# Conditioning loads on GpSimd's queue and a reordered recurrence stage in a two-layer hybrid decoder trunk

## The chip, the cores and the metric

The kernel runs on one core of one Trainium2 chip. The metric is the time of one execution on the device in microseconds; the time of a kernel is the median of its runs.

## The reference

Two layers, each of three sub-layers: a half-step SwiGLU FFN, a token mixer, another half-step FFN. Layer 0 mixes with HGRN2 (a gated linear recurrence), layer 1 with a chunked causal gMLP. Every sub-layer is wrapped by a norm before and after, with shift, scale and gate from a conditioning vector c. All is float32; SEQ is 256, D_MODEL 1024, D_FF 2816.

```python
def sublayer(x, fn, pre_g, post_g, shift, scale, gate, res_w):
    h = rms_norm(x, pre_g) * (1.0 + scale) + shift
    return x + res_w * gate * rms_norm(fn(h), post_g)

def swiglu(h, w_in, w_out):
    a, b = jnp.split(h @ w_in, 2, axis=-1)
    return (jax.nn.silu(a) * b) @ w_out

def hgrn2_mix(h, w_in, w_out, out_norm, lb):
    q, f, i, g = jnp.split(h @ w_in, [HG_F, 2 * HG_F, 2 * HG_F + D_MODEL], axis=-1)
    q = jax.nn.silu(q)
    log_f = jnp.logaddexp(jnp.log(lb), jnp.log1p(-lb) + jax.nn.log_sigmoid(f))
    k = (1.0 - lb) * jax.nn.sigmoid(-f)
    # S_t = diag(f_t) S_{t-1} + k_t i_t^T,  o_t = S_t^T q_t, in chunks, 8 heads of 128
    ...
    o = rms_norm(o, out_norm) * jax.nn.silu(g)          # per head
    return o.reshape(B, S, D_MODEL) @ w_out

cond = jax.nn.silu(c)
mod = cond @ ada_w[i] + ada_b[i]      # per layer: 9 x 1024 shifts, scales and gates
```

## The kernel before

**Weights.** They come in 188 blocks of 128x2048 float32 (1 MB), in the order in which they are used. `wblock` (L112) loads a block in two halves into `raw` tiles over SP's queue and splits it into a high part (cast on ScalarE, L119) and a low part (subtraction on VectorE, L120), both in the float32r format; each product of full precision is then three TensorE products of high and low parts (`mm3`, `mm3f`, `chunk2`). Six split blocks fit in the pool `whl` (12 tiles), which in the recurrence stage also holds the gate `gg`, the values `v`, the keys `kn` and the decays with queries `bq`.

**Conditioning.** `ada_w` is 144 tiles of 128x1024 (512 KB). `ada` (L159) loads each and reduces it against `cond` on VectorE (L169) into a column of `mod`. The loads go through `self.load` (L55), which writes them into SP's queue in program order between the weight halves; `pace` sets how many go with each block. Their buffers are the pool `adap` (two tiles), and for the first 16 also four tiles of `p4`. The norm gate of a sub-layer (`gate_tile`, L188) is the only user of GpSimd's (POOL's) queue: a row is stored to DRAM and read back to all partitions, `gflat` and `G`, once for each of the six sub-layers.

**Order on the engines.** The kernel is written in program order; the build's planner then orders each engine's instructions by when it takes their inputs to be ready, earlier program text first, and gives out buffers. What must not move is tied by hand: `keep_in_program_order` ties an instruction to the one traced before it on its engine, and `paced` ties a product behind the one named in `self.gate`.

**FFNs.** The first accumulates block by block as its conditioned input appears (L418). The other three begin with two units in token-major form (`proj`, split order, L291 to L294, then `post_tok`: silu, product, transposes L396, split into `gT`), and run nine further units of 256 columns (`unit2`, `chunk2`, L328 and L329), with the output products (`out_unit`, L142 to L144) of a unit two behind them.

**The recurrence stage, `hgrn`.** The projections come in this order: first half of the gate with the first half of the values (`proj`), queries and forget gates of the first four heads (`feat`, L334 to L336), then, as fill between the steps of the first four heads' recurrence, queries and forget gates of the other four and the second half of the values (`tok`). `gate_f` (L524) turns a forget projection into log decays and keys, a chain between ScalarE and VectorE with a scratch tile `L` from the pool `adap`. `attn` (L551) is the recurrence of four heads in nine steps: the diagonal scores (L559), seven levels of block size 64 down to 1 (operands L582, L587, L593 on VectorE with an exponential between, scores L599, merge L570), and the products with the values (L632, L634). `zip_steps` puts one step of the fill behind each step of `attn`. `finish` (L639) norms the heads of a half (squares with a sum per head on ScalarE, L645; scaling and gating per head on VectorE, L658), transposes them (L663) and splits them for the output products. The second half of the gate is projected as fill of the second `attn`.

## Time and profile before

| | us |
|---|---|
| runs, median of 3 | 1191.67 (1189.63 to 1193.36) |
| the profiled execution | 1193.24, span 1191.5 |
| TensorE busy | 1146.5 |
| VectorE busy | 888.8 |
| ScalarE busy | 657.2 |
| GpSimd busy | 6.8 |
| idle VectorE ended by a conditioning load | 91.5 (51 times) |
| issue to landing, conditioning load on SP's queue, median | 6.5 |
| mean granted TensorE clock | 0.984 |

The stages by the trace: first FFN to about 218 us, recurrence 218 to 386, second FFN to 575, third to 770, gMLP to 1000, last FFN to the end. In the views PE is TensorE's products, PEld its weight loads, DVE VectorE, ACT ScalarE, POOL GpSimd, SP the queue that issues loads; L120 is line 120 of the kernel. A row of waits names who waited for whom, with total, times and longest in us. A matmul's busy time includes its overlap with the next one.

### The profile page before, as it was taken

The page shows a single profiled execution, that of the slowest core. Times are in us where ns is not written, and L with a number is a line of the kernel's source. Part 1 is how long each engine was busy: PE and PEld are TensorE (multiplying, and loading weights), DVE is VectorE, ACT ScalarE, POOL GpSimd, SP SyncE. Part 2 cuts the span into 40 slices and gives each one's busy share as a digit, 9 for nine tenths or more (in the row PEclk, how much of TensorE's full clock was granted, in tenths as well). Part 3 has the DMA queues.
Part 4 walks back from the last instruction along what each step waited for, and adds up shares of the span by engine and source line. Part 5 has one row for each costly group of instructions (what it writes and reads, how often), then busy time and mean ns, then how long its engine had stood idle before and what let it go on. Part 6 is the DMA issues. An engine that isn't in the chain of part 4 may idle for free.

```text
span 1191.5 us, 17180 instructions
## 1 busy us (share of the span) xinstructions
PE 1146.5 (96%) x6518; PEld 995.4 (84%) x6518; DVE 888.8 (75%) x1331; ACT 657.2 (55%) x1054; POOL 6.8 (1%) x16
## 2 busy tenths in 40 slices
PE   7999999997997999999999999999999999999997
PEld 6999998797895788888778888888888887888886
DVE  6997888868887887787677787657978786666652
ACT  6464446648766754456655545554754457555541
POOL 0000000000000000000000000000000000000000
PEclk9999999997999999999999999999999999999999
DMA  9899998782335777887578888537777765666640
GB/s 345 311 314 318 333 327 314 251 285 101 124 95 185 263 267 272 278 272 262 173 251 267 282 269 272 188 124 261 277 254 262 248 212 177 203 222 233 213 137 36
DMA packets 79765, 282.32 MB, mean 237 GB/s; under 512 B 9873, under 2 KB 10561, under 8 KB 79682
## 3 DMA queue, kind: packets, MB, share of 16 engines
q1 hardware_dynamic: 78626, 278.05, 68.0%
q0 software_dynamic: 1056, 3.17, 0.8%
q8 instruction: 51, 0.84, 0.3%
q14 instruction: 32, 0.26, 0.1%
HBM read 280.11 MB, written 1.07 MB: 236 GB/s over the span
## 4 chain that ended last, share of the span: by engine, by line
PE 73%; DMA 10%; DVE 8%; ACT 5%; issue 3%; SPq 0%; DVEq 0%; ACTq 0%
PE ups L328 15%; PE ups L329 8%; PE y L144 7%; PE y L142 7%; PE y L143 7%; PE ups L418 4%; DMA ada<-in_ada 4%; DMA raw<-in_wffn 4%; DVE w L120 3%; PE ups L334 3%; PE ups L336 3%; PE ups L335 3%; DMA raw<-in_whg 3%; ACT w L119 2%; PE ab L599 2%
## 5 line engine op out<-in xcount | busy, mean ns | idle before, releaser
L120 DVE TENSOR_TENSOR w<-raw,w 128x1024 fp32r<-128x1024 f32 x376 | 453.5, 1220 | 84.7 <-ACT w L119 77.5
L119 ACT CAST w<-raw 128x1024 fp32r<-128x1024 f32 x376 | 388.0, 1050 | 202.9 <-DMA raw<-in_wffn 79.4
L328 PE MATMUL ups<-h,w 128*128 128x512 f32 x864 | 303.1, 394 | 0.0
L169 DVE CUSTOM_DVE_ANT_0 junkv<-ada,cond 128x1024 bf16<-128x1024 f32 x144 | 175.8, 1221 | 92.0 <-DMA ada<-in_ada 91.5
L329 PE MATMUL ups<-h,w 128*128 128x256 f32 x864 | 242.5, 281 | 0.0
L328 PEld LDWEIGHTS ups<-h,w 128*128 128x128 f32 x864 | 162.3, 188 | 36.8
L142 PE MATMUL y<-w,t 128*128 128x512 f32 x448 | 179.4, 400 | 4.5 <-ACT t L147 4.5
L143 PE MATMUL y<-w,t 128*128 128x512 f32 x448 | 178.2, 398 | 0.0
L144 PE MATMUL y<-w,t 128*128 128x512 f32 x448 | 177.6, 397 | 0.2
L329 PEld LDWEIGHTS ups<-h,w 128*128 128x128 f32 x864 | 163.7, 190 | 0.9
L334 PE MATMUL ups<-h,w 128*128 128x256 f32 x416 | 118.3, 285 | 0.6 <-ACT w L119 0.6
L336 PE MATMUL ups<-h,w 128*128 128x256 f32 x416 | 117.8, 283 | 0.2 <-DVE w L120 0.2
L335 PE MATMUL ups<-h,w 128*128 128x256 f32 x416 | 117.6, 283 | 0.0
L142 PEld LDWEIGHTS y<-w,t 128*128 128x128 f32 x448 | 84.5, 189 | 24.1 <-ACT t L147 5.3
L144 PEld LDWEIGHTS y<-w,t 128*128 128x128 f32 x448 | 84.3, 189 | 21.0 <-DVE t L148 1.1
L143 PEld LDWEIGHTS y<-w,t 128*128 128x128 f32 x448 | 84.5, 189 | 17.9
L79 ACT ACTIVATE t<-t 128x256 f32<-128x256 f32 (+2 forms) x70 | 36.3, 523 | 97.7 <-DVE t L378 95.5
L334 PEld LDWEIGHTS ups<-h,w 128*128 128x128 f32 x416 | 79.7, 192 | 1.7 <-ACT w L119 0.8
L335 PEld LDWEIGHTS ups<-h,w 128*128 128x128 f32 x416 | 79.7, 192 | 0.8 <-issue 0.2
L336 PEld LDWEIGHTS ups<-h,w 128*128 128x128 f32 x416 | 79.7, 192 | 0.4 <-DVE w L120 0.4
L291 PE MATMUL pps<-w,h 128*128 128x512 f32 x160 | 64.4, 403 | 5.3 <-DVE h L247 5.3
L292 PE MATMUL pps<-w,h 128*128 128x512 f32 x160 | 63.8, 399 | 0.0
(199 smaller groups left out, 1435.4 us busy)
## 6 DMA issues: line engine op xcount, KB each, us to landing
raw<-in_wffn SPq DMA_DIRECT2D x264, 512.0 KB, 5.5
ada<-in_ada SPq DMA_DIRECT2D x144, 512.0 KB, 6.5
raw<-in_wgmu SPq DMA_DIRECT2D x48, 512.0 KB, 5.2
raw<-in_whg SPq DMA_DIRECT2D x40, 512.0 KB, 5.8
raw<-in_wgmv SPq DMA_DIRECT2D x24, 512.0 KB, 5.0
G<-gflat POOLq DMA_DIRECT2D x6, 512.0 KB, 5.9
t<-in_gbin SPq DMA_DIRECT2D x6, 256.0 KB, 5.2
x<-in_x SPq DMA_DIRECT2D x2, 512.0 KB, 4.0
```

Of the source, the lines that this page charges most:

```text
L119: nc.scalar.copy(hi[:, sl], raw)
L120: nc.vector.tensor_sub(lo[:, sl], raw, hi[:, sl])
L142: self.paced(mm(ps, l[0], r[0], start=start, stop=False))
L143: mm(ps, l[0], r[1], start=False, stop=False)
L144: mm(ps, l[1], r[0], start=False, stop=stop)
L169: nc.vector.tensor_tensor_reduce(junk, t, self.cond, 1.0, 0.0, ALU.mult, ALU.add, self.mod[i // 24][:, i % 24:i % 24 + 1])
L291: mm(res[g][t], h(0, kc), u(0, kc), start=kc == 0, stop=False)
L328: self.paced(mm(ps, u[0], self.h2[:, :, :, kc, :], start=kc == 0, stop=False))
L329: mm(ps[:, 1, :], u[1], self.h2[:, 0, :, kc, :], start=False, stop=kc == KC - 1)
L334: self.paced(mm(o, u[0], h[0], start=start, stop=False))
L335: mm(o, u[0], h[1], start=False, stop=False)
L336: mm(o, u[1], h[0], start=False, stop=stop)
```

## The change

- The conditioning loads are issued on GpSimd's queue, tied to the order of that queue. `adap` has three tiles. The scratch `L` of `gate_f` has a tile of its own for one pair of heads and uses the tile `hf` for the other.
- `pace` spreads the loads over 22, 23 and 27 blocks where it spread them over 25, 26 and 30; in the later FFNs it is set before `post_tok`.
- In the later FFNs the first half of the first `unit2` is written between the two token tiles of `post_tok`, and each group of output products is tied behind the last unit product.
- In the recurrence stage both halves of the gate are projected first, with silu at eviction; then the forget gate of the first four heads; then the queries of all eight. The first recurrence is filled with half of the first values, the other forget gate, the rest of the first values and a quarter of the second values, two steps ahead; the second with the rest of the values and the output products. The weight blocks are laid out in that order, and the step behind the diagonal scores is tied behind them.
- `finish` squares a whole bank, sums the four heads of it on VectorE, multiplies with the gate before the norm's factor is known, and scales by that factor per head.

```diff
-        self.adap = pool("adap", 2)
+        self.adap = pool("adap", 3)
+        self.lp = pool("lp", 1)
...
-            self.load(t, self.d["ada"][i])
+            self.tc.keep_in_program_order(nc.gpsimd.dma_start(t, self.d["ada"][i]))
...
     def out_unit(self, y, gT, wo, first):
         for t in range(NT):
             for h in range(2):
+                self.gate = self.last
...
         def post_tok(pa, pb):
             gTs = [self.gtile() for _ in range(2)]
+            pend.extend(gTs)
...
-            return gTs
+                yield
...
-            pend = post_tok(*self.proj(hT, [wa, wb], 512, split=True))
+            pend = []
+            self.pace(bg, 23)
+            tokens = post_tok(*self.proj(hT, [wa, wb], 512, split=True))
+            next(tokens)
+            steps = unit2(nb(), nb())
+            next(steps)
+            next(tokens)
...
-            L = self.adap.tile([P, 512], F32, tag="ada", name="L")
+            L = self.lp.tile([P, 512], F32, tag="L", name="L") if pr else self.scr.tile([P, 512], F32, tag="hf", name="L")
...
         def finish(hb, ops, sqrt=False):
...
             for u in range(2):
-                for i in range(4):
-                    junk = self.scr.tile([P, 512], BF16, tag="junka", name="junka")
-                    nc.scalar.activation(junk[:, 0:P], o4[u][:, i, :], AF.Square, accum_out=ss[:, 4 * u + i:4 * u + i + 1])
+                o3 = ops[u].rearrange("p t h v -> p (t h) v")
+                sq = self.t2().rearrange("p (i v) -> p i v", i=4)
+                nc.scalar.activation(sq, o3, AF.Square)
+                c0 = 2 * (2 * hb + u) * P
+                nc.vector.tensor_mul(og[:, 512 * u:512 * u + 512].rearrange("p (t c) -> p t c", t=NT),
+                                     ops[u].rearrange("p t h v -> p t (h v)"), gg[:, :, c0:c0 + 2 * P])
+                nc.vector.reduce_sum(ss[:, 4 * u:4 * u + 4], sq, axis=mybir.AxisListType.X)
...
                 for i in range(4):
-                    t, c0 = i // 2, (2 * pair + i % 2) * P
-                    nc.vector.scalar_tensor_tensor(on[:, i, :], o4[u][:, i, :], r[:, 4 * u + i:4 * u + i + 1],
-                                                   gg[:, t, c0:c0 + P], op0=ALU.mult, op1=ALU.mult)
+                    nc.vector.tensor_scalar(on[:, i, :], on[:, i, :], r[:, 4 * u + i:4 * u + i + 1], None, op0=ALU.mult)
...
         for t in range(NT):
-            self.tact(gg[:, t, 0:512], pg[0][t], AF.Silu)
-            nc.scalar.copy(v[:, t, 0:512], pg[1][t])
+            for g in range(2):
+                self.tact(gg[:, t, 512 * g:512 * g + 512], pg[g][t], AF.Silu)
...
-        run(feat(lambda pr, ps: self.tact(qs(0, pr), ps, AF.Silu)))
         self.table("natural_log_exp_and_others")
         self.hg_cols()
         run(feat(lambda pr, ps: gate_f(0, pr, ps)))
+        self.table("silu_and_others")
+        for hb in range(2):
+            run(feat(lambda pr, ps: self.tact(qs(hb, pr), ps, AF.Silu)))
+        self.table("natural_log_exp_and_others")
...
         zip_steps(attn(0, bank_y, ops[0]), [
-            feat(lambda pr, ps: nc.scalar.copy(qs(1, pr), ps)), once(q1_silu),
-            feat(lambda pr, ps: gate_f(1, pr, ps)),
-            tok(lambda t, ps: nc.scalar.copy(v[:, t, 512:], ps))], 5)
+            once(v0), once(v0), feat(lambda pr, ps: gate_f(1, pr, ps)), v0, once(v1)], 2)
...
         def outs():
             finish(0, ops[0])
             yield
+            yield
...
-        zip_steps(attn(1, bank_a, ops[1]), [
-            tok(lambda t, ps: nc.scalar.copy(gg[:, t, 512:], ps)), outs()], 0)
+        zip_steps(attn(1, bank_a, ops[1]), [v1, outs()], 0)
         y = state["y"]
-        self.table("silu_and_others")
-        g_silu(1)
```

More of the change, by code (lines that the diff above doesn't have):

```diff
@@ L328, in chunk2 @@
             self.paced(mm(ps, u[0], self.h2[:, :, :, kc, :], start=kc == 0, stop=False))
-            mm(ps[:, 1, :], u[1], self.h2[:, 0, :, kc, :], start=False, stop=kc == KC - 1)
+            self.last = mm(ps[:, 1, :], u[1], self.h2[:, 0, :, kc, :], start=False, stop=kc == KC - 1)
         return ps
@@ L335, in mm3f @@
         mm(o, u[0], h[1], start=False, stop=False)
-        mm(o, u[1], h[0], start=False, stop=stop)
+        self.last = mm(o, u[1], h[0], start=False, stop=stop)
     def gtile(self):
@@ L434, in ffn @@
             else:
-                steps = unit2(nb(), nb())
-                next(steps)
+                if u > 2:
+                    steps = unit2(nb(), nb())
+                    next(steps)
                 next(steps)
@@ L558, in attn @@
                     c = slice(512 * u + i * P, 512 * u + (i + 1) * P)
-                    nc.tensor.matmul(ps[:, i * P:(i + 1) * P], k[:, c], q[:, c], start=True, stop=True)
+                    score = nc.tensor.matmul(ps[:, i * P:(i + 1) * P], k[:, c], q[:, c], start=True, stop=True)
+                self.gate = score
                 nc.vector.tensor_mul(St[:, 512 * u:512 * u + 512].rearrange("p (i t) -> p i t", i=4),
@@ L679, in bank_a, with once @@
             return self.acc.tile([P, 512], F32, tag="acc", name="ab")
-        def g_silu(g):
-            o = gg[:, :, g * 512:(g + 1) * 512]
-            self.tact(o, o, AF.Silu)
-        def once(fn):
-            fn()
-            return
-            yield
+        def once(gen):
+            yield next(gen)
         def run(*gens):
@@ L1056, in _layout @@
     bl = []
-    for c0 in (3072, 2048, 0, 1024, 512, 1536, 2560, 3584):
-        bl += [_blk(hw, (512 * h, 512), (c0, 512)) for h in range(2)]
+    for c0, h in ((3072, 0), (3072, 1), (3584, 0), (3584, 1), (1024, 0), (1024, 1), (0, 0), (0, 1), (512, 0), (512, 1),
+                  (2048, 0), (1536, 0), (1536, 1), (2048, 1), (2560, 0), (2560, 1)):
+        bl.append(_blk(hw, (512 * h, 512), (c0, 512)))
     bl += [_blk(ho, (256 * u, 256), (0, D)) for u in range(4)]
```

22 lines of the change are left out of this document (10 added, 12 removed).

## The prediction

> **What bounds the kernel now.** I read the page first: engine totals, then the chain that ended last.
>
> ```profile
> span 1191.5 us, 17180 instructions
> PE 1146.5 (96%) x6518; PEld 995.4 (84%) x6518; DVE 888.8 (75%) x1331; ACT 657.2 (55%) x1054; POOL 6.8 (1%) x16
> PE 73%; DMA 10%; DVE 8%; ACT 5%; issue 3%; SPq 0%; DVEq 0%; ACTq 0%
> ```
>
> TensorE is busy for 96% of the span and carries 73% of the chain. The change leaves its number of products nearly as it is, so the gain can come only from the 45 us in which PE stands, and from stretches in which it runs at half clock. The second view is therefore PE's waits, over hgrn (260 to 375 us) and then over what follows (400 to 1030 us).
>
> ```profile
> PE ots L663 <- DVE t L658: 4.4, 1, 4.4
> PE fps L336 <- DVE w L120: 3.1, 2, 1.7
> PE ab L599 <- DVE t L593: 3.0, 1, 3.0
> PE fps L334 <- ACT w L119: 0.7, 1, 0.7
> PE ab L634 <- DVE t L570: 0.5, 1, 0.5
> ...
> PE y L142 <- ACT t L147: 4.5, 3, 2.4
> PE tps L396 <- DVE t L393: 0.9, 1, 0.9
> ```
>
> The columns are: who waited for whom, microseconds in total, times, longest. The first five rows are the recurrence's stage; the last two are the token-major start of the three later FFNs, one wait each. The third view cuts the span into stretches (PE, PEld, DVE, ACT, POOL busy, then granted clock, DMA share, GB/s).
>
> ```profile
> 0.00:16.00 16.00, 7.43 (x21) 4.44 (x21) 6.79 (x17) 10.51 (x16) 0.20 (x4) 1.00 0.87 317
> 16.00:64.00 48.00, 48.00 (x383) 47.62 (x384) 43.86 (x71) 25.84 (x37) 0.00 (x0) 0.96 0.91 324
> 64.00:163.00 99.00, 99.00 (x692) 92.35 (x691) 80.96 (x107) 48.25 (x55) 0.78 (x2) 1.00 0.92 327
> 314.00:364.00 50.00, 49.38 (x328) 44.05 (x326) 42.20 (x70) 33.26 (x69) 0.12 (x1) 1.00 0.36 118
> ...
> 273.20:280.05 6.85, 5.50 (x26) 5.50 (x27) 5.84 (x10) 6.74 (x13) 0.00 (x0) 0.50 0.64 227
> 286.87:293.70 6.83, 6.83 (x34) 6.83 (x34) 3.83 (x9) 6.03 (x16) 0.00 (x0) 0.50 0.26 85
> 363.50:372.20 8.70, 4.17 (x14) 2.61 (x13) 6.79 (x16) 6.33 (x13) 0.00 (x0) 0.80 0.73 250
> ```
>
> The first FFN (16 to 163 us) has PE full and the DMA engines at 0.91: nothing can be won there, only lost. Inside hgrn two stretches after idle PE time ran at clock 0.50, and a third has a mean of 0.80.
>
> **The change, what it should take away.** A: gate, forget and query order. Today the first forget gate's ACT and VectorE work falls beside query products of the second half, and its scratch tile L shares the two conditioning buffers:
>
> ```profile
> ACT L L529 <- DVE mod L169: 3.9, 1, 3.9
> SPq L56 <- DVE mod L169: 77.2, 42, 6.2
> ```
>
> SP, whose queue carries the weights too, stood 77.2 us for conditioning buffers; that goes, and where PE is full it brings nothing. ACT stood 3.9 us for a conditioning reduction to free L, and weight casts (L119) queue behind it on ACT, L120 behind them, PE behind those. After the change L has buffers of its own, two query products (2 x 96 products of 256 columns, at 48.0/383 = 0.125 us, 24 us) follow the first gate as cover, and the level-64 operands are ready before the scores. So the waits of 3.1, 0.7 and 3.0 go: 6.8 us. The half-clock stretches behind them: 26 and 34 products at 0.125 would take 3.25 and 4.25 us where 5.50 and 6.83 were busy, 4.8 us. A = 11.6 us. What is late next is VectorE in the recurrence, costed under F.
>
> B: whole-bank output norm before the last products.
>
> ```profile
> L645 ACT ACTIVATE junka<-ab x16: 251/278/280, 327.0 to 365.1; 128x128 bf16<-128x128 f32 x16
> L645 ACT ACTIVATION_READ_ACCUMULATOR junka<-ab x16: 186/194/205, 327.1 to 365.3; 128x1 f32 x16
> L658 DVE SCALAR_TENSOR_TENSOR t<-ab,r,w x16: 337/342/353, 342.4 to 369.6; 128x128 f32<-128x128 f32 x16
> L393 DVE TENSOR_TENSOR t<-t,pps 128x512 f32<-128x512 f32 x6 | 4.1, 680 | 0.6 <-PE pps L294 0.6
> L79 ACT ACTIVATE t<-pps 128x512 f32<-128x512 f32 x6 | 3.5, 587 | 0.0
> L233 DVE TENSOR_SCALAR xn<-x,r 128x512 f32<-128x512 f32 x10 | 4.8, 485 | 0.3
> ```
>
> Of the stretch 363.5 to 372.2 us, 14 products need about 2.4 us at full clock (6 of 512 columns at twice 0.125, 8 transposes at 0.11, the pitch of the small scores under F); 6.3 us are lost. Eight squares with their accumulator reads, 8 x (0.278 + 0.194) = 3.8 us on ACT, become two of 0.59. VectorE gets two products of 0.68, two reductions, and eight scalings of 128x128 instead of eight of 0.342. No row shows such a reduction: bounds 0.485 (L233) and 0.68 (L393), taken 0.68 because it reads as L393 does, a whole bank at one element a step. A 128x128 scaling lies between a quarter of L233 (0.12) and L658 (0.342); taken 0.25. The path to the first transpose is then one square 0.59, one reduction 0.68, three column operations of 0.2, four scalings 1.0: 2.9 us, with one weight cast and one subtraction possibly ahead (1.05 + 1.22) 5.2. PE has 12 output products (3.0 us) beside it, so 0 to 2.2 us of idleness stay, plus an ACT pass of 0.59 that evicts the transposes; I take 1.8. B = 6.3 - 1.8 = 4.5 us (bounds 3.5 to 5.7). The table switch and the second half's gate silu that stood ahead of it on ACT go too; ACT was covered there, so I give nothing for them.
>
> C: FFN starts. Output products that ran ahead of their order (L142 waiting for L147) are now held behind the last unit product, and the first half unit of the next block (16 products of 512 columns and 16 of 256, 6.0 us) fills between the two token halves. 4.5 + 0.9 = 5.4 us; I leave 0.4 for what stays. C = 5.0 us.
>
> **What it adds.** The 144 conditioning loads leave SP's queue for POOL's, behind the norm-gate transfers only.
>
> ```profile
> L169 DVE CUSTOM_DVE_ANT_0 junkv<-ada,cond 128x1024 bf16<-128x1024 f32 x144 | 175.8, 1221 | 92.0 <-DMA ada<-in_ada 91.5
> L461 DVE TENSOR_TENSOR lb_m<-lb x1: 156/156/156, 70.8 to 70.8; 128x8 f32<-128x8 f32 x1
> L201 POOL DMA_DIRECT2D G<-gflat x6: 550/551/560, 162.9 to 1140.0; - x6
> DMA to landing us min/median/max: 3.5/6.5/11.1
> DMA to landing us min/median/max: 4.3/5.9/7.5
> 263.00:380.00 117.00, 0.66 (x1) 0.93 0.41 139
> 380.00:537.00 157.00, 33.01 (x27) 0.98 0.76 261
> ```
>
> L461 belongs to hgrn and ran at 70.8 us, as soon as its input was there: the build's planner runs ahead whatever is ready. The loads were paced because SP's queue is written in order. On POOL each waits only for one of three buffers and for the POOL instruction before it, so they will run in bursts, each burst stopped by the next gate's pair of transfers (POOL stands there for the landing, 4 to 7 us, and the loads behind it with it; no reduction is due then). Issue costs 144 x 0.55 = 79 us of a POOL that is 1% busy. The last two rows are the reductions alone: 27 lie in 380 to 537 us; by the code's counts 24 of those are issued between the second and the third gate's transfers and can now start at about 315 us, inside the second recurrence.
>
> D, start: the loads compete with x. Up to seven (four ring, three own buffers) leave at once; x and constants are 1.16 MB, at 317 GB/s 3.7 us, and if both queues take turns the second x lands up to 3.7 us late, against about 1.5 us of slack (issued within the first 2 us and 4.0 to landing, so near 6; used at 7.55). PE at 16 to 64 us is full, so a late start stays. Bounds 0 and 3.7; I take 1.2, nearest the row of the use.
>
> ```profile
> x<-in_x SPq DMA_DIRECT2D x2, 512.0 KB, 4.0
> ...
> 6.32 1.22 DVE xn L905
> 7.55 1.14 DVE yg L905
> ```
>
> The Trainium skill, page "DMA: Bandwidth & Descriptors", section "Rules for kernel authors", speaks against this part: issuing from several engines gives no bandwidth, since all share 16 DMA engines. With that rule D is the 1.2 us taken; were the queues independent it would be 0 and the sum 1.2 lower. The share of 0.87 at the start agrees with the rule.
>
> E, bursts in the second recurrence: 24 reductions want 24 x 1.30 = 31 us where VectorE has 50.0 - 42.2 = 7.8 us idle, so about six fit, each pushing the next VectorE instruction by up to 1.3 us. Bounds -1 (those six no longer stand in the next stage) and 7.8; PE has fill there, so I take 2.
>
> F, the recurrence itself: per level VectorE does
>
> ```profile
> L582 DVE TENSOR_TENSOR t<-w 128x512 f32<-128x512 f32 x12 | 8.2, 683 | 0.2 <-issue 0.2
> L593 DVE TENSOR_TENSOR t<-t,w 128x512 f32<-128x512 f32 x14 | 9.7, 690 | 0.2 <-ACT t L79 0.2
> L570 DVE COPY_PREDICATED t<-lmask,ab 128x512 f32<-128x512 int32 x14 | 12.5, 893 | 4.9 <-PE ab L599 4.9
> 295.09 1.73 PE ab L599 x16
> ```
>
> twice 0.68, 0.69, 0.89: 2.9 us, against 1.7 of scores. Counting the steps of both fillers, the second recurrence has one filled level fewer (1.2 us), and the new norm of the first half adds 2 x 0.68 + 2 x 0.68 + 8 x (0.25 - 0.342) = 2.0 us of VectorE there. Bounds 0 (the idle 7.8 us takes it) and 8 (the whole norm exposed); I take 3.2.
>
> G, transitions: the burst behind the third gate (from 537 us) reaches the turn at 560 to 580 us, whose VectorE chain is short operations that each can wait 1.3 us. Bounds 0 and 8 (six such steps); taken 1.5. The bursts in the first FFN cost nothing as long as weights lead: VectorE has 18 us idle in 64 to 163 us, and the count of reductions there does not change. If that cover is gone, each load delays a cast by up to 1.3 us.
>
> Pacing numbers change which block carries a load; on POOL they bind no more. Cost 0. Three tables instead of four switches on ACT: covered, 0.
>
> **Sum.** The profiled execution took 1193.2 us for its span of 1191.5. 1193.2 - 11.6 - 4.5 - 5.0 + 1.2 + 2.0 + 3.2 + 1.5 = 1180.0. That execution lies 1.6 us above the median of the runs, 1191.7; against the median that is 1178.4, and I say 1178.5.
>
> **Rivals.** R1: the gap moves into the recurrence. VectorE is 84% busy at 314 to 364 us, its dearer norm and the early reductions meet there; PE then waits at the unfilled levels. E and F at their upper ends, 7.8 + 8 in place of 2.0 + 3.2, and nothing else changed: 1190.6 by the profile, 1189.0 against the median. For it: VectorE's busy share; against: PE waited only 0.5 us there. It lies on both sides of the 0.3% (3.6 us) that is about what a measurement can tell.
>
> R2, slower: reductions wait in VectorE's queue for loads that land later than planned, and L120 waits behind them. VectorE is idle for 302.7 us, 91.5 of it already behind such loads: 211 us of slack over 128 loads after the start, so it decides from 1.65 us of added lateness a load; at 1.8 us PE loses 128 x 1.8 - 211 = 19 us: 1197.5. Against it: POOL's own transfers land in 5.9 us where SP's conditioning loads take 6.5, and 512 KB both. The Trainium skill, page "SBUF — State Buffer", section "SBUF: two separate sides", would back R2: DMAs issued from POOL wait for their descriptors while VectorE runs copies or scalings in a two-port mode. The six POOL transfers in this trace show no such delay, so I give it no more for that.
>
> R3: the change does not do what it says: bursts do not form or the waits only change names, and gains and costs cancel: 1191.
>
> **How the numbers follow.** Forecast (1170 to 1187 as its own range) 0.62; R1 0.18, half of it faster; R2 0.13; R3 0.07. Faster by over 0.3%: 0.62 + 0.09 + 0.01 = 0.72; within: 0.08 + 0.06 = 0.14; slower: 0.01 + 0.13 = 0.14. The low end is every gain at no cost, 1191.7 - 21.1 - 1.8 = 1168.8; the high end takes in R1, R3 and most of R2: 1168 to 1196.
>
> **What would show it.** A: no PE wait on L120 or L593 in hgrn and clock 1.00 from the gate products to the recurrence's end. B: the wait of the `ots` transposes under 2 us. C: no `y` wait on L147. D: the first L418 product after 16.0 us. E and G: reductions (L169 today) between 315 and 380 us, and more of them at 540 to 580. R1 shows as PE waits on L570 or L593 after 300 us, R2 as VectorE's wait for `ada` over 200 us. The prediction falls if hgrn keeps its length, or if weights starve PE in the first FFN.

## The result: slower, and the profile after

| | before | changed |
|---|---|---|
| median of 4 runs, us | 1191.17 (1189.63 to 1193.36) | 1261.16 (1260.15 to 1266.05) |
| ratio to before, 95% | | 1.0594 [1.0562, 1.0627] |
| profiled execution, us | 1193.24 | 1260.15 |

The forecast was 1178.5 us, between 1168 and 1196. The page of the changed kernel, in the order in which the page of before was read:

```profile
span 1258.4 us, 17248 instructions
PE 1162.6 (92%) x6518; PEld 1005.0 (80%) x6518; DVE 890.3 (71%) x1339; ACT 655.3 (52%) x1023; POOL 82.5 (7%) x160
PE 63%; issue 14%; DMA 13%; DVE 6%; ACT 2%; POOL 1%; SPq 0%; DVEq 0%; POOLq 0%; ACTq 0%
PE ups L329 13%; DMA ada<-in_ada 10%; PE ups L330 7%; PE y L143 6%; PE y L144 5%; PE y L145 5%; PE ups L422 4%; PE ups L335 2%; DMA raw<-in_wffn 2%; PE ups L336 2%; PE ups L337 2%; DVE w L121 2%; PE pps L292 2%; PE pps L293 2%; PE pps L295 1%
L170 DVE CUSTOM_DVE_ANT_0 junkv<-ada,cond 128x1024 bf16<-128x1024 f32 x144 | 175.8, 1221 | 50.4 <-DMA ada<-in_ada 49.5
```

VectorE and ScalarE have no more work: 890.3 us against 888.8, and 655.3 against 657.2. GpSimd's 82.5 us, against 6.8, are the issues of the loads. TensorE stands idle for 95.8 us of the span where it was 45.0, and its 16 us of added busy time go with a granted clock of 0.970 against 0.984. The chain names the new item: conditioning loads, `ada`, are 10% of it, where they were 4%. Yet VectorE's idle time behind these loads, in the last row, has fallen from 91.5 to 49.5 us. Both are right. What counts is where a wait lies, and these are the places:

```profile
PE ots L678 <- DVE t L674: 13.5, 2, 8.2
PE pps L292 <- DVE h L248: 2.9, 1, 2.9
PE pps L292 <- DVE r L225: 2.9, 1, 2.9
...
PE vps L859 <- ACT w L857: 7.9, 1, 7.9
PE vps L859 <- DVE t L866: 6.5, 4, 3.4
PE ups L329 <- DVE t L149: 6.3, 2, 3.4
PE npa L240 <- ACT xn L236: 4.5, 2, 4.0
```

These are TensorE's waits, first from 245 to 420 us, then from 420 to 1080. All are turns of the program: a norm, a transition, the start of an FFN, the gMLP's first value products. At each, TensorE's next products hang on a chain of short steps on VectorE or ScalarE. VectorE's order in time at one such place, the inverse square root of the gMLP's norm (columns: start, duration, engine, line, what; in brackets the idle time before it and its cause):

```profile
899.26 1.22 DVE L121 TENSOR_TENSOR w<-raw,w 128x1024 fp32r<-128x1024 f32 x1
900.40 0.21 DVE L96 SCALAR_TENSOR_TENSOR rs_q<-rs_y,rs_hv 128x1 f32<-128x1 f32 x1
903.96 1.23 DVE L170 CUSTOM_DVE_ANT_0 junkv<-ada,cond 128x1024 bf16<-128x1024 f32 x1 [3.36 <-DMA ada<-in_ada]
905.11 0.08 DVE L170 DVE_READ_ACCUMULATOR2_ANT mod<- 128x1 f32 x1
905.11 0.15 DVE L101 SCALAR_TENSOR_TENSOR rs_y<-rs_q,rs_y 128x1 f32<-128x1 f32 x1
907.32 1.23 DVE L121 TENSOR_TENSOR w<-raw,w 128x1024 fp32r<-128x1024 f32 x1 [2.05 <-ACT w L120]
908.46 0.21 DVE L96 SCALAR_TENSOR_TENSOR rs_q<-rs_y,rs_hv 128x1 f32<-128x1 f32 x1
```

```profile
906.25 1.04 ACT L120 CAST w<-raw 128x1024 fp32r<-128x1024 f32 x1 [6.51 <-DMA raw<-in_wgmu]
```

A step of 0.15 us (L101, 905.11) whose input was there at 900.6 waits 4.5 us, because a reduction stands ahead of it in VectorE's queue and its load has not landed. ScalarE meanwhile stands 6.51 us for a weight half. The `vps` products then wait 7.9 us. The load came late twice over. It was issued at 894.75, the first of three back to back, when a wait of 100.8 us for the gate's row had ended on GpSimd's queue; and it landed only near 904. GpSimd's row, and the stretch from 901 to 903 us (length, PE, PEld, DVE, ACT, POOL busy, granted clock, DMA share, GB/s):

```profile
894.75 1.57 POOL L168 DMA_DIRECT2D ada<-in_ada  x3
901.00:903.00 2.00, 2.00 (x19) 2.00 (x18) 0.00 (x0) 0.00 (x0) 0.00 (x0) 1.00 1.03 420
```

The DMA engines are full there, and from 890 to 925 us a weight half took up to 12.2 us to land and a conditioning load up to 13.3; at the same turn before (836 to 872 us) these were 6.8 and 7.2. The median over the run, 6.1 us for a conditioning load against 6.5 before, shows nothing of it.

### The profile page after: what moved, and what is told of

The parts are those of the page before. It is cut to its first block, busy times and chain, and to the rows that moved or that the text cites. A ratio compares the mean times of both kernels' runs of the same rounds, so it can differ in the third digit from the quotient of the medians.

```text
span 1258.4 us, 17248 instructions
## 1 busy us (share of the span) xinstructions
PE 1162.6 (92%) x6518; PEld 1005.0 (80%) x6518; DVE 890.3 (71%) x1339; ACT 655.3 (52%) x1023; POOL 82.5 (7%) x160
## 4 chain that ended last, share of the span: by engine, by line
PE 63%; issue 14%; DMA 13%; DVE 6%; ACT 2%; POOL 1%; SPq 0%; DVEq 0%; POOLq 0%; ACTq 0%
PE ups L329 13%; DMA ada<-in_ada 10%; PE ups L330 7%; PE y L143 6%; PE y L144 5%; PE y L145 5%; PE ups L422 4%; PE ups L335 2%; DMA raw<-in_wffn 2%; PE ups L336 2%; PE ups L337 2%; DVE w L121 2%; PE pps L292 2%; PE pps L293 2%; PE pps L295 1%
## 5 line engine op out<-in xcount | busy, mean ns | idle before, releaser
L120 ACT CAST w<-raw 128x1024 fp32r<-128x1024 f32 x376 | 386.6, 1050 | 305.5 <-DMA raw<-in_wffn 90.9
L329 PE MATMUL ups<-h,w 128*128 128x512 f32 x864 | 306.5, 398 | 7.5 <-DVE t L149 7.5
L170 DVE CUSTOM_DVE_ANT_0 junkv<-ada,cond 128x1024 bf16<-128x1024 f32 x144 | 175.8, 1221 | 50.4 <-DMA ada<-in_ada 49.5
L329 PEld LDWEIGHTS ups<-h,w 128*128 128x128 f32 x864 | 163.5, 189 | 46.7 <-issue 8.4
L330 PEld LDWEIGHTS ups<-h,w 128*128 128x128 f32 x864 | 164.3, 190 | 0.9
L143 PEld LDWEIGHTS y<-w,t 128*128 128x128 f32 x448 | 85.4, 191 | 26.1 <-ACT t L148 6.7
L168 POOL DMA_DIRECT2D ada<-in_ada x144 | 76.0, 530 | 446.0 <-DVE mod L170 312.2
L145 PEld LDWEIGHTS y<-w,t 128*128 128x128 f32 x448 | 85.4, 191 | 22.5 <-DVE t L149 2.2
L144 PEld LDWEIGHTS y<-w,t 128*128 128x128 f32 x448 | 85.5, 191 | 18.3
L335 PEld LDWEIGHTS ups<-h,w 128*128 128x128 f32 x416 | 81.4, 196 | 7.4 <-ACT t L80 5.7
L336 PEld LDWEIGHTS ups<-h,w 128*128 128x128 f32 x416 | 81.5, 196 | 0.8 <-issue 0.2
L337 PEld LDWEIGHTS ups<-h,w 128*128 128x128 f32 x416 | 81.3, 195 | 0.4 <-DVE w L121 0.4
```

Source lines behind the costliest of these rows:

```text
L120: nc.scalar.copy(hi[:, sl], raw)
L143: self.paced(mm(ps, l[0], r[0], start=start, stop=False))
L144: mm(ps, l[0], r[1], start=False, stop=False)
L145: mm(ps, l[1], r[0], start=False, stop=stop)
L170: nc.vector.tensor_tensor_reduce(junk, t, self.cond, 1.0, 0.0, ALU.mult, ALU.add, self.mod[i // 24][:, i % 24:i % 24 + 1])
L329: self.paced(mm(ps, u[0], self.h2[:, :, :, kc, :], start=kc == 0, stop=False))
```

## The experiments

All times are medians; "before" ran beside each and gave 1190.6 to 1192.7 us. The first table sums the runs; the second has the parts of some of them, from the start of one transition's `npa` transposes to the next (the first from the first product of the first FFN, the last to the last product), as the profiled executions show them.

| kernel | us | ratio to before, 95% |
|---|---|---|
| changed, loads on SP | 1201.02 | 1.0070 [1.0049, 1.0091] |
| before, loads on POOL | 1269.79 | 1.0644 [1.0603, 1.0684] |
| changed, reductions in order | 1218.87 | 1.0224 [1.0186, 1.0262] |
| before, FFN edit | 1203.66 | 1.0087 [1.0058, 1.0116] |
| before, output hold | 1197.61 | 1.0053 [1.0033, 1.0073] |
| before, token split and pace | 1195.64 | 1.0042 [1.0015, 1.0069] |
| before, pace 22 | 1197.23 | 1.0053 [1.0036, 1.0071] |
| loads on SP, no FFN edit | 1186.85 | 0.9971 [0.9947, 0.9995] |
| the same, norm per head | 1185.34 | 0.9945 [0.9917, 0.9974] |
| the same, whole-bank norm in two steps | 1185.59 | 0.9953 [0.9937, 0.9969] |
| the same, norm per head in two steps | 1182.16 | 0.9914 [0.9883, 0.9945] |
| changed, gate transfers on ScalarE's queue | 1264.46 | 1.0612 [1.0579, 1.0646] |
| changed, short reductions | 1278.37 | 1.0735 [1.0658, 1.0813] |
| the same, loads on SP | 1200.75 | 1.0082 [1.0058, 1.0106] |
| changed, short loads | 1218.12 | 1.0215 [1.0194, 1.0235] |
| the same, loads on SP | 1204.84 | 1.0093 [1.0059, 1.0127] |
| changed, two buffers | 1281.92 | 1.0759 [1.0724, 1.0794] |
| changed, loads two ahead | 1217.97 | 1.0235 [1.0195, 1.0274] |

| part, us | start | FFN 0 | hgrn | FFN 1 | FFN 2 | gMLP | FFN 3 |
|---|---|---|---|---|---|---|---|
| before | 16.0 | 188.7 | 178.9 | 193.2 | 193.8 | 220.8 | 193.4 |
| changed | 21.5 | 208.3 | 186.2 | 204.5 | 199.8 | 236.7 | 194.7 |
| loads on SP | 16.0 | 191.5 | 179.2 | 195.0 | 192.7 | 220.6 | 196.4 |
| reductions in order | 19.3 | 200.2 | 176.1 | 192.4 | 194.6 | 229.4 | 197.5 |
| gate transfers on ScalarE's queue | 21.0 | 228.2 | 195.6 | 199.3 | 194.5 | 220.4 | 195.7 |

### Which edit

Theories: the loads' new queue makes bunches of reductions that cost; the other edits cost; the loads' transfers cost. The loads back in SP's queue:

```diff
-            self.tc.keep_in_program_order(nc.gpsimd.dma_start(t, self.d["ada"][i]))
+            self.load(t, self.d["ada"][i])
```

> The changed kernel with its 144 conditioning loads put back into SyncE's queue, all else as changed. Theory 1, bursts: on GpSimd's queue the loads start when a buffer is free, so the planner has several tiles at once to reduce, and the reductions (1.25 us each) go into VectorE's order in bunches ahead of short steps that TensorE waits for; that costs about 80 us, and the other edits together gain some 10. Then this kernel takes 1165 to 1195 us, the reductions are spaced out between weight subtractions, and TensorE's waits of 8.72 us at the start (xps), 8.19 us at 366 us (ots) and 7.88 us at 914 us (vps) are below 3 us. Theory 2, the other edits (later first output products and tokens transposed later in the FFNs, the whole-bank norm) cost the time and the queue nothing: 1245 to 1262 us. Theory 3, the queue is at fault but by its transfers, which take the DMA engines at times at which weights are due, not by the reductions' order: 1165 to 1195 us here too; the third kernel parts it from theory 1.

1201.0 us: the one line is 60.1 of the 70 us. The rest, 9.5 us, is a loss too, where a gain had been expected: 6 us more than the upper end given. The `xps` wait fell to 3.6 us, what before has, the `vps` wait to 1.1, the `ots` wait (8.19 us at 366) only to 4.6. The same line alone in the kernel before:

> The kernel before with only the one line changed: the conditioning loads on GpSimd's queue (two buffers, shared with the lower-bound tile L, as before). Theory 1 (bursts) and theory 3 (transfers): slower than before by 40 to 90 us, 1230 to 1280 us, with bunches of three and more reductions in a row at the start, in the transitions and in the gated MLP. Theory 2 (the other edits): within 10 us of before, 1185 to 1200 us.

1269.8 us, +78.3. The queue costs with and without the other edits. Now the changed kernel with the reductions tied:

```diff
-            nc.vector.tensor_tensor_reduce(junk, t, self.cond, ...
+            self.tc.keep_in_program_order(nc.vector.tensor_tensor_reduce(junk, t, self.cond, ...
```

> The changed kernel, loads still on GpSimd's queue, but each reduction held in the program's order against the other instructions held so; by the instruction order that results, most reductions then stand singly or in pairs between weight subtractions, where the changed kernel has up to six in a row. Theory 1 (bursts): most of the loss goes, 1180 to 1215 us. Theory 3 (transfers on that queue cost, whatever the reductions' order): stays at 1240 us or above, with weights late (ScalarE's casts wait for raw) as in the changed kernel. Theory 2 (the other edits): stays at 1250 to 1265 us.

1218.9 us: with the queue as changed, the order of VectorE's instructions alone gives back 42 of the 60 us, not all; the time is 4 us above the upper end given for theory 1. The `vps` wait, the example above, did not go:

```profile
PE vps L859 <- ACT w L857: 8.2, 1, 8.2
```

There a reduction still waits 2.3 us for its load in front of the same short steps, and ScalarE 5.8 us for a weight half. The FFN edit alone:

> The kernel before with the FFN edit alone: an output unit's products held behind the unit products issued last before it, token tiles transposed one after the other with the next unit's first half between, and the pace set 23 and 22 blocks wide. Loads on SyncE's queue. By the prediction's step for this edit: a gain of about 5 us, 1186 us. Theory 1 or 3: within 8 us of before, 1180 to 1196 us. Theory 2: slower by 15 to 45 us, 1206 to 1236 us, with waits of the unit products for y's or the units' sums that before does not have.

1203.7 us: it costs 12.1 us, under what theory 2 asked for and above theory 1's bound. There are new waits, which these rows of TensorE's waits from 390 to 1060 us show, where before has a `y` wait of 4.5 us and a `tps` wait of 0.9:

```profile
PE ups L328 <- DVE t L148: 8.7, 3, 3.1
PE tps L399 <- DVE t L396: 5.1, 3, 1.7
```

### The edits beside the queue

The loads on SP's queue, and the FFN edit's lines put back:

> The changed kernel with the conditioning loads on SyncE's queue and with the FFN edit undone; the hgrn part's new block order, the whole-bank norm and the gated MLP's pace stay. If the parts add up, it is the 1201.0 us of the kernel with the loads on SyncE's queue less the 12.1 us that the FFN edit alone cost: 1189 us (1184 to 1194), that is, the hgrn part's edits gain about 3 us. By the prediction's sum for the hgrn part (A and B gained, F and G paid: 11.4 us) it would be 1180 us. If the FFN edit's loss belongs to the kernel before's layout alone, and the hgrn part loses by itself: 1197 to 1203 us.

1186.9 us: the parts add up, and the hgrn edits gain 4.7 us where 11.4 net were forecast. The FFN edit in halves; first the hold:

```diff
+                self.gate = self.last      # in out_unit
```

> The kernel before with one half of the FFN edit: an output unit's products are held behind the last unit product, the pace and the token transposes stay as before. The loss of the FFN edit alone was 12.1 us, of which 8.0 lay in the first FFN (196.7 us against 188.7 from its first product to its first norm transpose), which has no token transposes. If the hold makes it: 1196 to 1203 us, with the first FFN some 5 us or more longer. If the pace or chance in the planner's order makes the first FFN's part: 1189 to 1194 us.

1197.6 us, as if the hold made it, but not where that theory put it: the first FFN keeps its length (188.8 us). The loss is in the later FFNs, where the output products that had filled the token transposes' wait are now held back:

```profile
PE tps L398 <- DVE t L395: 12.0, 3, 4.4
```

> The kernel before with the other half of the FFN edit: the two token tiles are transposed one after the other with half a unit between, and the pace is set 23 and 22 blocks wide; output units aren't held. The kernel with the whole FFN edit shows in each of the three later FFNs a wait of 2.1 to 3.1 us of a unit's product for the gate tile's subtraction (line 148) and one of 1.8 to 2.0 us of the second tile's transposes, where before has one wait of 1.5 to 2.6 us. If the split makes these: three times 2 to 3 us more, 1197 to 1201 us. If the hold does (nothing fills the wait, since output products stand behind): no change, 1188 to 1194 us.

1195.6 us: both numbers given missed. The first FFN takes 194.3 us, where the pace is the only edit, and the waits of the three later FFNs come to 5.4 us, what before has. So one number was tried alone:

```diff
-        self.pace(bg, 25 if f == 0 else 26)
+        self.pace(bg, 22 if f == 0 else 26)
```

> The kernel before with one number changed: in the first FFN the conditioning loads are spread over 22 weight blocks instead of 25. With the token split alone the first FFN, which has no token tiles and where this number is the only edit, took 194.3 us against 188.7; with the hold alone, which leaves the number, 188.8. If the pace is the cause: the first FFN again near 194 us (192 to 197), with the first pre-norm's transposes and the gate's column late, and the whole 1194 to 1199 us. If the 5.6 us were the planner's answer to another edit: 188 to 190 us there, 1189 to 1194 us in all.

1197.2 us, first FFN 194.6: the pace is the cause. TensorE's waits from 195 to 235 us, this kernel first, then before:

```profile
PE npa L239 <- ACT xn L235: 3.7, 1, 3.7
PE pps L291 <- DVE gate L193: 3.4, 1, 3.4
PE pps L291 <- DVE h L247: 1.8, 1, 1.8
```

```profile
PE pps L291 <- DVE h L247: 2.3, 1, 2.3
PE npa L239 <- ACT xn L235: 1.2, 1, 1.2
```

The split itself (4.1 less 5.9 us) is nothing that the intervals can tell from zero. Then the kernel without the FFN edit, with the lines of the whole-bank norm put back to the norm per head:

> The changed kernel with the loads on SyncE's queue, the FFN edit undone and the output norm per head as before; only the hgrn part's block order, the values as fill, its empty step and the gated MLP's pace are left. With the loads on SyncE's queue the changed kernel shows a new wait of 4.75 us of the output transposes for the norm of the first half at 333 us, followed by 13.7 us at the half clock, about 11.6 us together. If the whole-bank norm makes it (all of the bank is squared, multiplied and reduced before one scale is known): it goes, and this kernel is 5 to 12 us faster than the one with the whole-bank norm, near 1180 us. If the place of the norm makes it (no fill is left between the first half's end and its transposes): it stays at 4 us or more and the time is within 4 us of the one with the whole-bank norm.

1185.3 us, within 4 us of the whole-bank norm, but the wait at 326 us fell from 4.6 to 1.8 us (the rows' values for the 4.75 and 1.97 us of the expectations): neither account is whole. The place was tried with both norms, the scaling and transposes one step of the recurrence behind the norm:

```diff
-            finish(0, ops[0])
-            yield
+            norm = finish(0, ops[0])    # stops ahead of the scalings
+            next(norm)
+            yield
+            run(norm)
             yield
```

> The kernel with the loads on SyncE's queue and without the FFN edit (1186.9 us), in which the first half's whole-bank norm is given out one step ahead of its scaling and transposes, with a step of the second recurrence between, instead of an empty step behind. There the transposes wait 4.75 us for the norm's scaling at 326 us, and 13.7 us at the half clock follow: about 11.6 us. If the wait is one of place (the transposes stand in TensorE's queue ahead of recurrence products that are ready): it falls below 1.5 us and the time to 1175 to 1182 us. If the recurrence has no product ready there either: the wait moves to the recurrence's products, and the time stays at 1183 to 1189 us.

> The same with the output norm per head, as the kernel before has it (its one-step form took 1185.3 us, with a wait of 1.97 us and 10.2 us at the half clock in this place): 1178 to 1183 us if the place makes the wait, 1183 to 1188 us if not. Between this kernel and the one with the whole-bank norm less than 4 us is expected: the whole-bank norm saved nothing that the traces show so far.

1185.6 and 1182.2 us. With the whole-bank norm the wait splits into 2.1 for a recurrence product and 2.6 for the transposes, 6.8 us are at the half clock instead of 13.7: the hgrn part fell from 175.7 to 170.3 us, but other parts grew and the time hardly moved. With the norm per head this wait is gone, and the recurrence runs almost without a gap:

```profile
225.00:349.00 124.00, 123.49 (x887) 114.98 (x888) 107.12 (x179) 87.15 (x159) 1.08 (x2) 1.00 0.51 171
```

Its hgrn part takes 167.1 us against 178.9, and it has the lowest median of the study, 0.9914 [0.9883, 0.9945] of before. By the hgrn parts of the four profiled executions both accounts hold, each for a share: 175.7 us with the whole-bank norm in one step, 172.0 per head, 170.3 and 167.1 in two steps. The norm per head is worth 3 to 4 us, the place about 5.

### What it is about the queue

GpSimd's queue in the changed kernel, longest waits first:

```profile
POOL gflat L200 <- ACT grow L198: 664.4, 6, 215.9
POOL ada L168 <- DVE mod L170: 312.2, 80, 34.8
```

The loads run as fast as buffers come free, then stand behind the next gate's row, and start again in a bunch when it has gone. Both transfers of the gate on ScalarE's queue:

```diff
-        nc.gpsimd.dma_start(flat, row)          # and G the same
+        nc.scalar.dma_start(flat, row)
```

> The changed kernel with the gate's two small transfers (its row to memory, and the row back to all partitions) issued from ScalarE's queue instead of GpSimd's. In the changed kernel GpSimd's queue waits 664.4 us in six places for the gate's row, with the later loads behind it; between two such waits the loads run as fast as their buffers come free, which puts the reductions' bunches right behind each gate, where the next transition lies. Without the waits all 144 loads are free to run ahead from the start. Theory 1 in this form (a bunch costs where TensorE's next work hangs on VectorE's short steps): the bunches move to the first two parts, none is left in the gated MLP's transition and after it, so the 15.9 us that the gated MLP lost (236.7 us against 220.8) and the 6.0 of the third FFN go, and the whole is 1215 to 1245 us. If the bunches cost where they are by their number alone, as VectorE's time: no change, 1255 to 1265 us. If the transfers are what costs: the first parts lose more than the later ones gain, 1260 us or more.

1264.5 us: the time fits the account by number and that of the transfers (1260 us or more), not the one given for theory 1; the parts did as theory 1 said. 113 of the 144 reductions fall before the second transition (75 in the changed kernel) and none after 565 us. The first two parts lose 29.3 us more, the gMLP is back at 220.4 us. The loss goes where the reductions go, and its sum stays. The gMLP's stretch in the changed kernel, then here:

```profile
820.30:1057.00 236.70, 221.52 (x1270) 191.97 (x1270) 172.42 (x272) 121.63 (x176) 13.15 (x25) 0.98 0.65 222
```

```profile
838.60:1059.00 220.40, 218.33 (x1269) 189.48 (x1269) 146.62 (x220) 121.10 (x176) 0.00 (x0) 1.00 0.55 183
```

And VectorE at the end of this kernel's first FFN, where TensorE stands 16.7 us for an FFN unit's result, whose product of the two halves is L370:

```profile
213.94 0.16 DVE L185 SCALAR_TENSOR_TENSOR A<-A,npre 128x8 f32<-128x8 f32 x1
215.34 1.23 DVE L170 CUSTOM_DVE_ANT_0 junkv<-ada,cond 128x1024 bf16<-128x1024 f32 x1 [1.24 <-DMA ada<-in_ada]
...
218.68 1.23 DVE L170 CUSTOM_DVE_ANT_0 junkv<-ada,cond 128x1024 bf16<-128x1024 f32 x1 [2.11 <-DMA ada<-in_ada]
...
223.71 1.22 DVE L170 CUSTOM_DVE_ANT_0 junkv<-ada,cond 128x1024 bf16<-128x1024 f32 x1
224.85 0.09 DVE L170 DVE_READ_ACCUMULATOR2_ANT mod<- 128x1 f32 x1
224.85 0.69 DVE L370 TENSOR_TENSOR t<-t,ups 128x512 f32<-128x512 f32 x1
```

Is it VectorE's time or the loads'? Each was cut to an eighth, on both queues. All four kernels leave out seven eighths of the conditioning's weights; with short loads the reduction keeps its length, by reading the 128 columns eight times:

```diff
-  tensor_tensor_reduce(junk, t, self.cond, ...)
+  tensor_tensor_reduce(junk[:, 0:P], t[:, 0:P], self.cond[:, 0:P], ...)      # short reductions
-  dma_start(t, self.d["ada"][i])
+  dma_start(t[:, 0:P], self.d["ada"][i][:, 0:P])                             # short loads
```

> The changed kernel (loads on GpSimd's queue) with each reduction over the first 128 of its 1024 columns; the loads stay whole. Seven eighths of the conditioning sums are left out. Beside it runs the same with the loads on SyncE's queue; whole, the two differ by 60.1 us (1261.2 against 1201.0). If VectorE's time in the bunches makes the difference (1.22 us a reduction, and steps that TensorE waits for behind up to eight of them): with short reductions the two differ by less than 20 us. If the loads do, by waits of the reductions for their tiles or by weights that land late: by 45 us or more.

> The pair's other half: loads on SyncE's queue, each reduction over 128 columns, the rest as in the changed kernel. Without some 130 us of VectorE's work that is spread over the run, little changes if that work is hidden there: 1190 to 1201 us.

> The changed kernel (loads on GpSimd's queue) with each load cut to its first 128 columns (64 KB for 512 KB), and the reduction run over these eight times, so that VectorE's work per reduction stays as it is; seven eighths of the conditioning's weights are left out. If VectorE's time in the bunches makes the difference between the two queues: it stays at 50 us or more, with this kernel at 1240 us or above. If the loads make it (their share of the DMA engines, and reductions that wait for tiles): the pair differs by less than 20 us. If both: 20 to 50 us.

> The pair's other half: loads of 64 KB on SyncE's queue, whole reductions over them, the rest as in the changed kernel: 1185 to 1201 us, since 66 MB fewer are moved and the weights come sooner in the first FFN.

With short reductions the queue costs 77.6 us (1278.4 against 1200.8), with short loads 13.3 (1218.1 against 1204.8). (Short loads on SP were to take 1201 us at most; they took 4 more.) That overturns the theory that VectorE's time in the bunches is what costs: nearly all of it is the loads. What stays with short loads lies in other places: the gMLP takes 222.8 us against 223.6 on SP, while the longest `ots` wait is 11.4 us against 4.6. With short reductions on POOL, VectorE waits where it had worked:

```profile
L170 DVE CUSTOM_DVE_ANT_0 junkv<-ada,cond 128x128 bf16<-128x128 f32 x144 | 41.6, 289 | 128.6 <-DMA ada<-in_ada 127.8
```

Two last runs on how; fewer buffers, and loads given out two tiles ahead, with the reductions tied as above:

```diff
-        self.adap = pool("adap", 3)             # two buffers
+        self.adap = pool("adap", 2)
...
-            (load of tile i, reduction of tile i)   # loads two ahead
+            (loads up to tile i + 2, reduction of tile i)
```

> The changed kernel with two buffers for the conditioning tiles instead of three (more than three found no room in SBUF). A load starts when the reduction two (now) or three (changed) tiles ahead has freed its buffer, and lands about 6 us later. If the loss is the reductions' wait for loads that start so late, with VectorE's later steps behind the waiting reduction: two buffers make it worse, 1266 to 1290 us. If the bunches' length counts (up to six in a row with three buffers, five with two): better, 1235 to 1258 us.

> The changed kernel, loads on GpSimd's queue, with each load given out two tiles ahead of its reduction and the reductions held in the program's order, so that a load has landed some weight blocks before its reduction comes up in VectorE's queue. If the wait of the reductions for their loads is what the queue costs: near the 1201.0 us of the loads on SyncE's queue (1196 to 1208), and below the 1218.9 us of the kernel with the reductions' order alone. If the loads' share of the DMA engines, taken from the weights, makes the remaining 18 us: no better than 1214 to 1224 us.

Two buffers start the loads later and move the same bytes: 1281.9 us, as the account of waiting reductions says. Loads two ahead (with the reductions in order): 1218.0, no better than the order alone and within the 1214 to 1224 us given for the loads' share of the DMA engines; the gMLP gains, 224.1 us against 229.4, and the second and third FFN lose that again. The chain by line of four kernels, in this order the loads on SP, reductions in order, two buffers, short reductions; only the `ada` share is to be read, 3%, 2%, 13%, 17%, beside 4% before and 10% changed:

```profile
PE ups L329 16%; PE ups L330 8%; PE y L143 8%; PE y L144 8%; PE y L145 8%; PE ups L422 4%; PE ups L336 4%; PE ups L337 4%; PE ups L335 4%; DMA ada<-in_ada 3%; DMA raw<-in_wffn 2%; DVE w L121 2%; PE ab L612 2%; DMA raw<-in_whg 2%; PE pps L292 1%
```

```profile
PE ups L329 16%; PE ups L330 8%; PE y L143 8%; PE y L144 8%; PE y L145 8%; DMA raw<-in_wffn 4%; PE ups L335 3%; PE ups L337 3%; PE ups L336 3%; DVE w L121 3%; DMA ada<-in_ada 2%; PE ab L612 2%; PE pps L292 2%; PE pps L293 2%; PE pps L295 2%
```

```profile
PE ups L329 13%; DMA ada<-in_ada 13%; PE ups L330 7%; PE y L143 6%; PE y L144 6%; PE y L145 6%; DMA raw<-in_wffn 5%; DVE w L121 4%; PE ups L335 2%; PE ups L336 2%; PE ups L337 2%; PE ab L612 2%; DVE junkv L170 2%; ACT w L120 1%; PE pps L292 1%
```

```profile
DMA ada<-in_ada 17%; PE ups L329 14%; PE ups L330 7%; PE y L143 7%; PE y L144 6%; PE y L145 6%; DMA raw<-in_wffn 3%; PE ups L335 3%; PE ups L336 2%; PE ups L337 2%; DVE w L121 2%; PE ab L612 2%; PE pps L292 2%; PE pps L293 2%; PE pps L295 1%
```

Order takes the waits for loads off the chain (2%), and 17 to 18 us remain. Against the loads on SP, the reductions in order lose 3.4 us at the start, 8.7 in the first FFN and 8.8 in the gMLP, and gain in the hgrn part and the FFN after it. In both kernels with the reductions in order the first product comes 3.4 us late, and ScalarE stands longer for FFN weights, 103.5 and 98.6 us, than with the loads on SP:

```profile
ACT w L120 <- DMA raw<-in_wffn: 67.6, 54, 3.2
```

At the gMLP's turn loads and weight halves land late, whatever the reductions' order (microseconds from issue to landing, median and longest):

| gMLP's turn | weight halves | conditioning loads |
|---|---|---|
| before, 836 to 872 us | 5.8, 6.8 | 6.6, 7.2 |
| changed, 890 to 925 us | 5.4, 12.2 | 6.7, 13.3 |
| reductions in order, 850 to 885 us | 7.0, 12.5 | 8.1, 13.3 |
| loads on SP, 840 to 875 us | 6.1, 6.7 | 7.0, 7.5 |

That points to the loads' share of the DMA engines, taken in bunches. It is not shown: no run takes it away with the order kept.

## Why the prediction was wrong, step by step

**The step that failed** is the one that prices the bursts, as E, G and "the bursts in the first FFN cost nothing", with rival R2. The bursts were foreseen, and where they start and stop. Their cost was taken as VectorE's time beyond its idle time, 3.5 us; changed against loads on SP, the queue costs 5.5 us at the start, 16.8 in the first FFN, 7.0, 9.5 and 7.1 in the next three parts, 16.1 in the gMLP, and gains 1.7 in the last FFN. E's own place came near: five reductions fall between 340 and 380 us where six were counted, and the `ots` wait there grew from 4.6 to 8.2 us. The loss is where nothing or 1.5 us was put: in the first FFN and at the turns. R2 named the right mechanism (reductions wait in VectorE's queue for late loads, and what follows waits behind them), at a chance of 0.13. It was priced wrongly: VectorE's idle time was summed over the whole run, 211 us of slack, as if slack in one place covered a wait in another. Its sign, `ada` waits over 200 us, failed for that reason too: they fell to 49.5 us while the time rose. At the median a load landed no later, 6.1 us against 6.5. Its issue was later, behind a buffer that the reduction before it frees (312.2 us of GpSimd's waits) or behind the gate's row; and where a bunch starts, the landing was later too, up to 13.3 us at the gMLP's turn. The prediction's argument against R2, landings over the whole run, could not see that.

**A, the forget order: right in its place, not in the total.** The waits for weights (L120) are gone from hgrn, and that for the level's operands (L593, now L606) is 0.3 us where it was 3.0. With the loads on SP, TensorE is busy for 105.12 of the 105.40 us up to the wait for the first half's norm, at full clock:

```profile
227.60:333.00 105.40, 105.12 (x760) 98.73 (x761) 87.59 (x142) 73.33 (x128) 1.07 (x2) 1.00 0.49 168
336.00:349.70 13.70, 11.82 (x48) 11.05 (x49) 12.10 (x27) 8.47 (x10) 0.00 (x0) 0.51 0.32 101
```

The second row is what took it back: 4.6 us of waiting for the first half's norm, and 13.7 us at 0.51 that begin within the wait, in which half of 11.8 busy us is lost: 10.5 us together, where A was 11.6.

**F** is thus the mis-sized term of this stage, 3.2 taken, its bound 8 ("the whole norm exposed") passed. R1 foresaw that the gap moves into the recurrence; it came on the `ots` transposes, not on L570 or L593. **B** did not come: the second `ots` wait is 3.9 us with the loads on SP and 5.3 in the changed kernel, 4.4 before, and with the norm per head the hgrn part is 3 to 4 us shorter.

**C** had the wrong sign: 5.0 gained was forecast, 12.1 lost was measured. Two of its claims fell. The `y` products that ran ahead were taken as the wait; they were its fill, and holding them costs 6.1 us. The pacing numbers were put at cost 0; with the loads on SP, 22 in place of 25 costs 5.9, and no run changes them alone with the loads on POOL.

**D** was 1.2, bounds 0 and 3.7; the first product came 5.5 us late. `x` was little of it: with the reductions in order its second half is used at 8.03 us, with the loads on SP at 7.42. Four reductions, at 7.57, 11.19, 12.65 and 13.91 us, stand among the steps of the first norm, and `adab`, 72 KB that the shifts and scales need, took 8.6 us to land where it takes 4.1 with the loads on SP. With the reductions in order two of the four are gone from there, `adab` still takes 8.5 us, and 3.4 of the 5.5 us stay. The landing of `adab` agrees with what the prediction cited from the Trainium skill ("DMA: Bandwidth & Descriptors", section "Rules for kernel authors"): another queue is no other bandwidth. The port rule cited for R2 ("SBUF — State Buffer", section "SBUF: two separate sides") does not show: loads on POOL landed in 6.1 us at the median, those on SP in 7.0 with the same other edits, and where landings were long, at the gMLP's turn, the DMA engines were full.

R3, that gains and costs cancel, did not come either: even with the loads on SP the edits lose 9.5 us. The range's low end, 1168.8 us, adds 1.8 us for which no row is given; B's own upper bound allows 1.2.

## What to carry to other kernels

In this kernel a transfer in the same queue as the weights was also a pace: taking it out freed the loads, and every reduction that the planner then placed by an assumed arrival stood in an in-order engine queue, in front of short steps that the next products needed. Price such a wait where it lies, at the norms and transitions, never against the engine's idle time as a whole, nor by the median landing of the run; and before holding work back, ask what it was filling. When the loads do move to another queue, tie their consumers to the program's order with it: here that was worth 42 of 60 us.

## What the hardware showed beyond that

In the recurrence a wait of TensorE cost more than its length. With the loads on SP the granted clock fell 2.6 us into the wait of 4.6 us and stayed at 0.51 for 13.7 us, 11.8 of them after the wait. In the changed kernel it fell 3.0 us into the wait of 8.2 us and stayed at 0.50 for 17.1 us, 11.9 of them after it. Two waits of 2.1 and 2.6 us brought 6.8 us, and with the norm per head the clock fell 1.3 us behind a wait of 1.8 us:

```profile
330.00:340.20 10.20, 10.20 (x43) 9.41 (x43) 7.78 (x10) 6.59 (x8) 0.00 (x0) 0.52 0.32 100
```

The Trainium skill, page "TensorE: Matmul & The Clock Gate", section "HAM oscillation — how this bites in real kernels", asks to keep idle gaps of TensorE below some 3.4 us. By that rule alone the 1.8 us should have been free; here they were not, in a recurrence whose products are small (128x64 around the wait).
